# A decoder trunk step on one core: own buffers for one weight stream, a longer load lead, other spacing of side work

## The chip, the core and the metric

The kernel runs on one core of a Trainium2 chip. The core has five engines with queues of their own: TensorE (PE in the profile; its weight loads are listed as PEld), VectorE (DVE), ScalarE (ACT), GpSimd (POOL) and SyncE (SP). Each queue runs in order: an instruction that waits for a semaphore holds up everything behind it on that queue. SP and POOL only start transfers here, apart from a few memsets on POOL. The metric is device microseconds of one execution, from three runs; lower is better.

## The reference

One layer of a hybrid decoder trunk, for 256 prompt tokens and 8 single sample tokens at a model width of 2048, all in float32. What is computed, cut down:

```python
mod = silu(c) @ w_ada + b_ada                    # 2048 x 12288: six vectors of 2048 for each of 9 rows
sh1, sc1, gt1, sh2, sc2, gt2 = split(mod, 6)
h = rmsnorm(x, g_pre_mix) * (1 + sc1) + sh1
z = h @ w_in                                     # 2048 x 15376
y_a = u * (W_s v + b)                            # causal 128x128 mixing, 8 groups
y_b = head_rmsnorm(recurrence(q, k, v, log_f)) * silu(hg)    # HGRN2, 8 heads of 128x128 state
y_c = head_rmsnorm(recurrence(q, k, v, log_a)) * silu(gr)    # GLA, 4 heads of 128x256 state
merged = sum over n of sigmoid(z_gate[n]) * (y_n @ w_branch[n])
x = x + gt1 * rmsnorm(merged @ w_out, g_post_mix)
h2 = rmsnorm(x, g_pre_mlp) * (1 + sc2) + sh2
x = x + gt2 * rmsnorm(square(relu(h2 @ w_mlp_up)) @ w_mlp_down, g_post_mlp)   # 2048 -> 8192 -> 2048
```

The prompt starts from zero states; each sample has its own old states (`state_hgrn`, `state_gla`), which are loaded, decayed, added to and stored again. The outputs are the new rows, the final states of the prompt, the updated states of the samples and the normalised v rows of the samples.

## The kernel before, in words

**Products.** Activations lie transposed, 128 channels by 264 columns (256 prompt tokens and 8 samples). Every float32 weight tile is split into a high part (`whi`, a cast on ScalarE, line 108) and a rest (`wlo`, a subtraction on VectorE, line 105), and each product is made as three TensorE products: high by high, high by low, low by high (lines 534 to 536). The weights are walked in blocks of 512 KB. The work on one block is a *granule*: 24 products of 128x128 weights with 264 columns. `linear` runs four granules (two for `w_branch`) into one accumulator of two PSUM banks, of which there are two (`new_acc`), and calls `background()` after each.

**The stream of weights.** `plan()` lists all blocks in the order of use, and `Stream` loads and splits them ahead: on each call of `ahead()` (lines 507 to 516) blocks up to `at + SPLIT_AHEAD` (2) are split and blocks up to `at + LOAD_AHEAD` (3) are loaded by SP into tiles of the pool tag `raw`, which has `RAW_BUFS` (6) buffers of 512 KB. There are six pairs of `whi`/`wlo` halves, three blocks' worth. Blocks 20 to 71 are loaded in pairs with longer rows (lines 483 to 493).

**The first projection.** `CHUNKS = (2, 2, 4, 4, 4)` cuts the 16 tiles of the inner dimension into five chunks, and for each chunk all 20 column groups are run (lines 660 to 687). In the first two chunks a granule covers two inner tiles and 512 columns, so it needs both accumulators at once; its result is copied out (chunk 0, line 672, ScalarE) or added (later chunks, line 674, VectorE). For each next chunk `First.paced` loads the modulation's weights for that chunk into tiles of another pool (`blk`, line 380), runs its small TensorE products (line 257) between granules, and makes the modulated activations.

**The rest of the modulation.** `ada_round(r)` (lines 271 to 299) makes one of the vectors of `mod`: 16 steps, each of them four 512-column products (line 287, eight records in the trace) on two tiles of 512 KB. The next step's two tiles are requested right after a step (line 288); they come from the same tag `raw` as the stream's blocks (line 278). Rounds 2, 3 and 4 run during the mixers. Round 5 runs between the output projection and the MLP, with 12 of its 32 tiles loaded early into other buffers (lines 1311 to 1319).

**Side work.** The mixers' work is written as Python generators which are advanced after each granule: `bg` (the recurrences of the prompt, `mixer_r`), `bs` (the samples' states, `samples_r`) and `ba` (the modulation). A rate says how many units each may advance in a granule (`RATES`, in the order bg, bs, ba). Products of the side work that read results of other engines are held back and put between two granules by `slot()` (lines 541 to 570): it takes noted `levels` and `samples` that were noted in an earlier granule, and one step of `ba` if that has credit (`owed`). `background()` opens a slot when `ba.owed` has reached 0.9, or when something noted waits and `ba` has credit, or when it has waited three granules.

**The samples.** `samples_r` (lines 927 to 975) has 8 steps for each of two HGRN2 groups and 16 for the GLA group. A step loads a 256 KB tile of states (`st`, line 942, four buffers) and a 256 KB broadcast of values (`vbc`, line 944, two buffers) through POOL, scales on ScalarE (line 959), adds on VectorE (line 961), stores (line 962) and leaves the tile for TensorE (line 561).

**Who sets the order.** TensorE, SP and POOL are issued in the order of the program text up to line 688; after line 811 TensorE and POOL are, and SP is ordered by a planner that puts an instruction into its queue when its model says that inputs and buffers are there, earlier program text first. ScalarE and VectorE are always ordered by that planner, and after line 1256 all engines are. Once planned, each queue is fixed.

Of the kernel before, what the change touches and what calls it, by code (L numbers as in the profile page):

```python
# [7 lines left out]
F32 = mybir.dt.float32  # L8
# [7 lines left out]
P = 128  # L16
# [4 lines left out]
NT = NP + NS  # L21
# [7 lines left out]

KC = 4  # L30
CW = 256
RAW_BUFS = 6
SPLIT_BUFS = 6
NBLK = 28
CHUNKS = (2, 2, 4, 4, 4)
RATES = ((1.6, 0.4, 0.36), (1.42, 0.4, 0.36), (1.2, 0.4, 0.36), (1.0, 0.4, 0.36))
ST_BUFS = 4
VB_BUFS = 2
N_PRE = 12
PRE_AT = (2, 3, 4, 5)  # L40
R0 = 0.34
ADA_BATCH = 4
ADA_LEAD = 3
PAIRED = 72
LOAD_AHEAD = 3
SPLIT_AHEAD = 2
N_BRANCH = 3
FILL = (5.0, 9.0)
# [2 lines left out]
SLOT_WAIT = 3  # L51
HELD_OWED = 1.0
LEVELS_HELD = 3


@with_exitstack
def hybrid_step_kernel(
# [9 lines left out]
    V, S, T = nc.vector, nc.scalar, nc.tensor  # L67
# [3 lines left out]
    rawp = ctx.enter_context(tc.tile_pool(name="rawp", bufs=RAW_BUFS))  # L71
# [9 lines left out]
    def nm(s):  # L81
        uid[0] += 1
        return f"{s}_{uid[0]}"
# [8 lines left out]
    def tmp(shape, tag, bufs=2):  # L92
        return tp.tile(shape, F32, tag=tag, name=nm(tag), bufs=bufs)
# [177 lines left out]
    def ada_round(r, pre=()):  # L271

        acc = pada.tile([P, 512], F32, tag="ada", name=nm("ada"))

        def load(n):
            if n < len(pre):
                return pre[n]
            w = rawp.tile([P, 1024], F32, tag="raw", name=nm("raw"))
            c0 = r * D + n % 2 * 1024
            nc.sync.dma_start(w, w_ada[0, n // 2 * P:(n // 2 + 1) * P, c0:c0 + 1024])  # L280
            return w

        ws = [load(0), load(1)]
        yield
        for k in range(KT):
            for j in range(4):
                T.matmul(acc[32 * j:32 * j + 32, :], cT[:, k, :], ws[j // 2][:, j % 2 * 512:j % 2 * 512 + 512], start=k == 0, stop=k == KT - 1)  # L287
# [12 lines left out]

    now = [0]
# [173 lines left out]
    class Stream:  # L475
# [5 lines left out]
        def load(self, i):  # L481
            w, k, n, c0, width = self.items[i]
            if i < PAIRED and n == 4:

                assert self.items[i + 1][1:4] == (k, n, c0 + width)
                self.raw[i], self.raw[i + 1] = [], []
                for h in range(2):
                    t = rawp.tile([P, 2, 2 * width], F32, tag="raw", name=nm("raw"))
                    r0 = (k + 2 * h) * P
                    nc.sync.dma_start(t, w[r0:r0 + 2 * P, c0:c0 + 2 * width].rearrange("(k p) c -> p k c", p=P))  # L490
                    self.raw[i].append(t[:, :, 0:width])
                    self.raw[i + 1].append(t[:, :, width:2 * width])
                return
            t = rawp.tile([P, n, width], F32, tag="raw", name=nm("raw"))
            nc.sync.dma_start(t, w[k * P:(k + n) * P, c0:c0 + width].rearrange("(k p) c -> p k c", p=P))
            self.raw[i] = [t[:, 0:n // 2, :], t[:, n // 2:n, :]]
# [28 lines left out]
    def granule(w, k0, n, c0, width, accs, xh, xl, k, first, last):  # L525

        item, parts = stream[0].next()
        assert item[1:] == (k0 + k, n, c0, width)
        h = n // 2
        for j in range(n):  # L530
            for m in range(width // P):
                o = accs[m // 2][:, m % 2, 0:NT]
                a, b = (p[:, j % h, m * P:(m + 1) * P] for p in parts[j // h])
                T.matmul(o, a, xh(k + j), start=first and j == 0, stop=False)  # L534
                T.matmul(o, a, xl(k + j), start=False, stop=False)  # L535
                T.matmul(o, b, xh(k + j), start=False, stop=last and j == n - 1)  # L536
        stream[0].ahead()

    levels, samples = [], []

    def slot():

        lv = [x for x in levels if x[0] < now[0]][:2]
        sv = [x for x in samples if x[0] < now[0]]
        del levels[:len(lv)]
        del samples[:len(sv)]
        if lv:
            pl = sm([P, 2, 8, 32])
            for i, (_, lhs, rhs, _) in enumerate(lv):
                for h in range(4):  # L550
                    for hf in range(2):
                        for b in range(4):
                            t0 = hf * P + b * 32
                            T.matmul(pl[32 * b:32 * b + 32, i, 2 * h + hf, :], lhs[:, h, t0:t0 + 32], rhs[:, h, t0:t0 + 32], start=True, stop=True)  # L554
        if sv:
            G, qm, os_ = sv[0][1]
            nh = 512 // G.dv
            po = sm([P, G.dv])
            for h in range(4):
                for i, (_, _, b, sts) in enumerate(sv):  # L560
                    T.matmul(po[32 * h:32 * h + 32, :], qm[:, h, b, :], sts[h // nh][:, h % nh, :], start=i == 0, stop=i == len(sv) - 1)
        if ba.g and ba.owed >= 0.0:
            ba.step()
        for i, (_, _, _, put) in enumerate(lv):
            put(pl[:, i])
        if sv:
            if sv[0][2] == 0:
                V.tensor_copy(os_, po)
            else:
                add(os_, os_, po)  # L570

    def background():

        now[0] += 1
        bg.pump(rate[0])
        bs.pump(rate[1])
        ba.owed = min(ba.owed + rate[2], SLOT_LATE) if ba.g else 0.0
        wait = now[0] - min([x[0] for x in levels + samples] + [now[0]])
        if ba.owed >= SLOT_LATE or wait and (ba.g and ba.owed >= 0.0 or wait >= SLOT_WAIT):
            slot()  # L580

# [345 lines left out]
    def samples_r(G):  # L927
# [10 lines left out]
        ahead = []  # L938
# [12 lines left out]
        sts = []  # L951
        for n, (b, h0) in enumerate(steps):
            if n + 2 < len(steps):

                yield lambda: len(sts) + sum(len(x[3]) for x in samples) <= ST_BUFS - 3
                fetch(*steps[n + 2])
            st, v = ahead.pop(0)
            for i in range(nh):
                S.activation(st[:, i, :], st[:, i, :], AF.Copy, scale=fs[:, h0 + i, b:b + 1])  # L959
            for i in range(nh):  # L960
# [311 lines left out]
    parts = []  # L1272
# [179 lines left out]
```

## Time and profile before

| | us |
|---|---|
| three runs: lowest, median, highest | 2011.64, 2017.7, 2018.89 |
| the profiled execution, device time | 2011.83 |
| its span, first to last instruction | 2010.0 |
| TensorE busy | 1932.7 (96%) |
| VectorE busy | 1191.7 (59%) |
| ScalarE busy | 996.0 (50%) |
| GpSimd busy | 85.5 (4%) |

The mean granted TensorE clock was 0.985 and 442.05 MB were moved, 220 GB/s over the span. The profile's page gives busy times, the span in 40 slices, DMA queues, the chain that ended last, groups of instructions by line, and DMA issues. Other views of the same trace list who waited for whom, instructions in order of time, and sums over stretches. The end of a TensorE product is modelled, so a busy TensorE may still run at less than its best rate: the number of products in a stretch says more than its busy time.

By the trace, the first projection runs from about 31 us to 320 us, the three branches with their side work to about 1110 us, the output projection to about 1209 us, and the MLP from about 1241 us to the end.

### The profile page before, as it was taken

To read this page: it belongs to the slowest core of one execution; us is meant where nothing else is said; L and a number is where in the kernel's file an instruction comes from. 1 tells how busy PE (TensorE), PEld (TensorE's weight loads), DVE (VectorE), ACT (ScalarE), POOL (GpSimd) and SP (SyncE) were. 2 spreads that over 40 slices of the span, in tenths; PEclk is the share of its full clock that TensorE was granted. 3 is DMA by queue.
4 is the path that set the end of the run, shared out by engine and by line. 5 is a ranking of instruction groups with operands and counts; after the bars stand their busy time and mean duration, and the time that the engine had idled before them with its cause. 6 is when DMAs were issued, how large, how long until landed. Compare 5 with 4: busy or idle time off the path is not lost.

```text
span 2010.0 us, 42078 instructions
## 1 busy us (share of the span) xinstructions
PE 1932.7 (96%) x16972; PEld 1820.7 (91%) x16972; DVE 1191.7 (59%) x2095; ACT 996.0 (50%) x1773; POOL 85.5 (4%) x128
## 2 busy tenths in 40 slices
PE   6999999989998999989999999999999999999997
PEld 4889999879987988779999995999999999999996
DVE  3466667667566576445655556555555555555666
ACT  5444354546665664454544545555444444454543
POOL 1000000111011011220000000000000000000000
PEclk8999999999999999999999999999999999999998
DMA  9796787788799679886755766755555555555552
GB/s 343 253 333 238 254 286 235 219 249 250 234 288 257 202 229 287 258 263 192 223 184 180 268 204 219 231 180 179 180 183 182 180 179 182 181 183 179 179 178 75
DMA packets 341267, 442.05 MB, mean 220 GB/s; under 512 B 14930, under 2 KB 285008, under 8 KB 341072
## 3 DMA queue, kind: packets, MB, share of 16 engines
q1 hardware_dynamic: 330880, 409.19, 62.6%
q0 software_dynamic: 9120, 28.91, 6.1%
q8 instruction: 133, 2.18, 0.4%
q10 hardware_dynamic: 1072, 1.25, 0.2%
q14 instruction: 62, 0.51, 0.1%
HBM read 427.60 MB, written 11.70 MB: 219 GB/s over the span
## 4 chain that ended last, share of the span: by engine, by line
PE 82%; DMA 6%; issue 3%; DVE 2%; ACT 1%; POOL 0%; DVEq 0%; ACTq 0%; POOLq 0%; SPq 0%
PE mm L534 25%; PE mm L535 25%; PE mm L536 25%; PE ada L287 3%; DMA raw<-in_w_in_dram 2%; DMA vbc<-vs_d 1%; PE ada L257 1%; DVE wlo L105 1%; PE sm L695 1%; DMA raw<-in_w_ada_dram 1%; PE sm L1063 1%; DMA st<-in_state_hgrn_dram 0%; ACT whi L108 0%; PE sm L554 0%; DMA raw<-in_w_branch_dram 0%
## 5 line engine op out<-in xcount | busy, mean ns | idle before, releaser
L534 PE MATMUL mm<-b,whi 128*128 128x264 f32 x4624 | 1328.9, 287 | 15.9 <-ACT whi L108 6.5
L535 PE MATMUL mm<-b,whi 128*128 128x264 f32 x4624 | 1319.8, 285 | 0.2 <-DVE b L105 0.2
L536 PE MATMUL mm<-b,wlo 128*128 128x264 f32 x4624 | 1316.8, 285 | 3.0 <-DVE wlo L105 2.9
L105 DVE TENSOR_TENSOR wlo<-raw,whi 128x512 fp32r<-128x512 f32 x1156 | 792.8, 690 | 649.7 <-ACT whi L108 644.7
L108 ACT CAST whi<-raw 128x512 fp32r<-128x512 f32 x1156 | 708.8, 618 | 843.0 <-PE mm L535 699.6
L534 PEld LDWEIGHTS mm<-b,whi 128*128 128x128 f32 x4624 | 874.0, 189 | 71.5 <-issue 30.2
L536 PEld LDWEIGHTS mm<-b,wlo 128*128 128x128 f32 x4624 | 873.5, 189 | 4.8 <-DVE wlo L105 4.7
L535 PEld LDWEIGHTS mm<-b,whi 128*128 128x128 f32 x4624 | 873.4, 189 | 2.3 <-DVE b L105 1.4
L102 DVE TENSOR_TENSOR b<-b,mm 128x528 f32<-128x528 f32 x136 | 95.4, 704 | 39.3 <-PE mm L536 39.1
L287 PE MATMUL ada<-raw,cT 128*32 128x512 f32 x464 | 75.7, 640 | 3.7 <-DMA raw<-in_w_ada_dram 3.7
L961 DVE SCALAR_TENSOR_TENSOR st<-vbc,b,st 128x128 f32<-128x128 f32 (+1 forms) x96 | 33.9, 392 | 52.4 <-DMA vbc<-vs_d 39.3
L959 ACT ACTIVATE st<-st,fs 128x128 f32<-128x128 f32 (+1 forms) x96 | 36.4, 430 | 44.9 <-DMA st<-in_state_gla_dram 26.9
L257 PE MATMUL ada<-b,cT 128*32 128x256 f32 (+1 forms) x640 | 36.4, 364 | 9.9 <-DMA b<-in_w_ada_dram 9.2
L257 PEld LDWEIGHTS ada<-b,cT 128*32 128x32 f32 x640 | 18.3, 116 | 22.9 <-DMA b<-in_w_ada_dram 7.6
L99 DVE TENSOR_TENSOR b<-b,b 128x512 f32<-128x512 f32 (+1 forms) x47 | 33.7, 744 | 1.7 <-ACT b L1024 0.7
L287 PEld LDWEIGHTS ada<-raw,cT 128*32 128x32 f32 x464 | 13.2, 113 | 16.8 <-DMA raw<-in_w_ada_dram 8.6
L944 POOL DMA_DIRECT2D vbc<-vs_d x32 | 24.1, 754 | 77.7 <-DVE st L961 45.5
L105 DVE TENSOR_TENSOR b<-gt,b 128x528 fp32r<-128x528 f32 x32 | 22.7, 709 | 3.7 <-ACT whi L108 0.5
L962 POOL DMA_DIRECT2D out_dram<-st x32 | 23.5, 734 | 30.6 <-DVE st L961 15.9
L99 DVE TENSOR_TENSOR gt<-vt 128x528 f32<-128x528 f32 x32 | 22.5, 702 | 0.0
L105 DVE TENSOR_TENSOR b<-b 128x1024 f32<-128x1024 f32 (+1 forms) x21 | 22.3, 1067 | 0.1
L554 PE MATMUL sm<-b 128*32 128x32 f32 x960 | 11.9, 205 | 10.3 <-DVE b L99 10.3
(283 smaller groups left out, 783.0 us busy)
## 6 DMA issues: line engine op xcount, KB each, us to landing
raw<-in_w_in_dram SPq DMA_DIRECT2D x242, 512.0 KB, 5.6
raw<-in_w_mlp_up_dram SPq DMA_DIRECT2D x128, 512.0 KB, 3.9
raw<-in_w_mlp_down_dram SPq DMA_DIRECT2D x128, 512.0 KB, 3.6
raw<-in_w_ada_dram SPq DMA_DIRECT2D x116, 512.0 KB, 4.7
b<-in_w_ada_dram SPq DMA_DIRECT2D x60, 512.0 KB, 7.5
raw<-in_w_branch_dram SPq DMA_DIRECT2D x48, 512.0 KB, 5.2
raw<-in_w_out_dram SPq DMA_DIRECT2D x32, 512.0 KB, 3.7
b<-in_w_ada_dram SPq DMA_DIRECT2D x32, 256.0 KB, 6.6
```

Source lines behind the costliest of these rows:

```text
L99: V.tensor_tensor(o, a, b, op=ALU.mult)
L102: V.tensor_tensor(o, a, b, op=ALU.add)
L105: V.tensor_tensor(o, a, b, op=ALU.subtract)
L108: S.copy(hi, src)
L257: T.matmul(acc[32 * j:32 * j + 32, 0:n], cT[:, k, :], w[:, n * j:n * j + n], start=k == 0, stop=k == KT - 1)
L287: T.matmul(acc[32 * j:32 * j + 32, :], cT[:, k, :], ws[j // 2][:, j % 2 * 512:j % 2 * 512 + 512], start=k == 0, stop=k == KT - 1)
L534: T.matmul(o, a, xh(k + j), start=first and j == 0, stop=False)
L535: T.matmul(o, a, xl(k + j), start=False, stop=False)
L536: T.matmul(o, b, xh(k + j), start=False, stop=last and j == n - 1)
L944: nc.gpsimd.dma_start(v, vs_d[G.i, h * nj:h * nj + 4, b, :].partition_broadcast(P))
L959: S.activation(st[:, i, :], st[:, i, :], AF.Copy, scale=fs[:, h0 + i, b:b + 1])
L961: V.scalar_tensor_tensor(st[:, i, :], v[:, i, :], k[:, h0 + i, NP + b:NP + b + 1], st[:, i, :], ALU.mult, ALU.add)
```

## The change

- The modulation's steps and (with `spare`) some of the paired stream loads get a tag of their own, `araw`, with two buffers; the stream's tag `raw` goes from six buffers to four.
- Blocks are requested five ahead of the current one, not three. Splitting stays two ahead.
- The third rate goes from 0.36 to 0.27 (from 0.34 to 0.30 in the last chunk of the first projection); the first rates go from 1.6 and 1.42 to 1.7 and 1.5.
- `granule` runs all of its products for one accumulator, then those for the other. This differs from before only where there are two, in the first two chunks.
- `slot` takes only what was noted at least two granules ago, and what it counts as waiting is shifted by one granule with it.
- In `samples_r` the states are still requested two steps ahead, the values now one step ahead and by a function of their own, and a step's use comes at least three granules after the later of its two requests.

```diff
-RAW_BUFS = 6
+RAW_BUFS = 4
+ADA_RAW = 2
...
-RATES = ((1.6, 0.4, 0.36), (1.42, 0.4, 0.36), (1.2, 0.4, 0.36), (1.0, 0.4, 0.36))
+RATES = ((1.7, 0.4, 0.27), (1.5, 0.4, 0.27), (1.2, 0.4, 0.27), (1.0, 0.4, 0.27))
...
-R0 = 0.34
+R0 = 0.3
...
-LOAD_AHEAD = 3
+LOAD_AHEAD = 5
...
+FETCHED = 3
+AGE = 2
...
@@ ada_round, load(n)
-            w = rawp.tile([P, 1024], F32, tag="raw", name=nm("raw"))
+            w = rawp.tile([P, 1024], F32, tag="araw", name=nm("araw"), bufs=ADA_RAW)
...
@@ Stream.load, paired blocks
+                spare = i % 6 == 4 and i < PAIRED - 20
                 for h in range(2):
-                    t = rawp.tile([P, 2, 2 * width], F32, tag="raw", name=nm("raw"))
+                    if spare:
+                        t = rawp.tile([P, 2, 2 * width], F32, tag="araw", name=nm("araw"), bufs=ADA_RAW)
+                    else:
+                        t = rawp.tile([P, 2, 2 * width], F32, tag="raw", name=nm("raw"))
...
@@ granule
-        for j in range(n):
-            for m in range(width // P):
-                o = accs[m // 2][:, m % 2, 0:NT]
+        for acc0, m0 in [(acc, 2 * i) for i, acc in enumerate(accs)]:
+            for j in range(n):
+                for m in range(m0, min(m0 + 2, width // P)):
+                    o = acc0[:, m % 2, 0:NT]
...
@@ slot
-        lv = [x for x in levels if x[0] < now[0]][:2]
-        sv = [x for x in samples if x[0] < now[0]]
+        lv = [x for x in levels if x[0] + AGE <= now[0]][:2]
+        sv = [x for x in samples if x[0] + AGE <= now[0]]
...
@@ background
-        wait = now[0] - min([x[0] for x in levels + samples] + [now[0]])
+        wait = max(now[0] + 1 - AGE - min([x[0] for x in levels + samples] + [now[0]]), 0)
...
@@ samples_r
         def fetch(b, h):
             st = tmp([P, nh, dv], "st", ST_BUFS)
             nc.gpsimd.dma_start(st, G.s_in(b, h, nh))
+            ahead.append((st, now[0]))
+
+        def values(b, h):
             v = tmp([P, 4, P], "vbc", VB_BUFS)
             nc.gpsimd.dma_start(v, vs_d[G.i, h * nj:h * nj + 4, b, :].partition_broadcast(P))
-            ahead.append((st, v.rearrange("p (h j) v -> p h (j v)", h=nh)))
+            vals.append((v.rearrange("p (h j) v -> p h (j v)", h=nh), now[0]))
...
+        values(*steps[0])
+        yield
...
                 fetch(*steps[n + 2])
-            st, v = ahead.pop(0)
+            if n + 1 < len(steps):
+                values(*steps[n + 1])
+            yield lambda: now[0] >= max(ahead[0][1], vals[0][1]) + FETCHED
+            st, v = ahead.pop(0)[0], vals.pop(0)[0]
```

More of the change, by code (lines that the diff above doesn't have):

```diff
@@ L529, in granule @@
         h = n // 2
-        for j in range(n):
-            for m in range(width // P):
-                o = accs[m // 2][:, m % 2, 0:NT]
[L533 to L536, printed above, removed]
+        for acc0, m0 in [(acc, 2 * i) for i, acc in enumerate(accs)]:
+            for j in range(n):
+                for m in range(m0, min(m0 + 2, width // P)):
+                    o = acc0[:, m % 2, 0:NT]
+                    a, b = (p[:, j % h, m * P:(m + 1) * P] for p in parts[j // h])
+                    T.matmul(o, a, xh(k + j), start=first and j == 0, stop=False)
+                    T.matmul(o, a, xl(k + j), start=False, stop=False)
+                    T.matmul(o, b, xh(k + j), start=False, stop=last and j == n - 1)
         stream[0].ahead()
@@ L937, in samples_r @@
         steps = [(b, h) for b in range(NS) for h in range(0, 4, nh)]
-        ahead = []
+        ahead, vals = [], []
         def fetch(b, h):
```

## The prediction

> **What bounds the kernel now.** I read the page's busy times first, then busy time by stretch, to find where TensorE runs at its full pace and where not; then TensorE's waits, and for each large one what held up the engine it waited for.
>
> ```profile
> span 2010.0 us, 42078 instructions
> ...
> PE 1932.7 (96%) x16972; PEld 1820.7 (91%) x16972; DVE 1191.7 (59%) x2095; ACT 996.0 (50%) x1773; POOL 85.5 (4%) x128
> ```
> ```profile
> 0.00:50.00 50.00, 31.15 (x268) 23.11 (x272) 18.62 (x59) 25.64 (x45) 6.48 (x16) 0.90 1.02 342
> ...
> 118.00:123.00 5.00, 5.00 (x31) 5.00 (x30) 2.61 (x4) 1.31 (x3) 0.00 (x0) 0.66 0.97 329
> 1300.00:1900.00 600.00, 600.00 (x4940) 600.00 (x4940) 344.31 (x510) 288.96 (x477) 0.00 (x0) 1.00 0.57 181
> ```
>
> The second fence gives, for a stretch: its length, busy time and count of PE, PEld, DVE, ACT, POOL, the granted clock, the DMA share and GB/s. From 1300 to 1900 us TensorE has no gap: 600/4940 = 0.1215 us for a product, 24 x 0.1215 = 2.92 us for a granule. Nothing in the change makes a product cheaper, so gains lie only in TensorE's waits, most of which fall before 960 us:
>
> ```profile
> PE sm L554 <- DVE b L99: 10.3, 2, 6.1
> PE sm L1149 <- ACT b L1151: 6.9, 1, 6.9
> PE mm L534 <- ACT whi L108: 6.5, 3, 4.2
> PE sm L561 <- ACT b L1089: 4.3, 1, 4.3
> PE mm L536 <- DVE wlo L105: 2.9, 6, 1.4
> PE sm L784 <- DVE srow L780: 2.2, 1, 2.2
> PE ada L287 <- DMA raw<-in_w_ada_dram: 1.5, 3, 0.8
> ```
>
> These are the waits from 300 to 960 us (total, times, longest), 34.6 us together. ScalarE and VectorE are half idle over the span, so why are they late? Their queues stand still behind transfers, as ScalarE's waits and its order of time in the same stretch show:
>
> ```profile
> ACT whi L108 <- DMA raw<-in_w_in_dram: 62.0, 22, 8.7
> ACT st L959 <- DMA st<-in_state_gla_dram: 26.9, 9, 5.6
> ACT st L959 <- DMA st<-in_state_hgrn_dram: 18.0, 8, 8.1
> ```
> ```profile
> 420.61 0.40 ACT L959 ACTIVATE st<-st,fs 128x128 f32<-128x128 f32 x1 [8.08 <-DMA st<-in_state_hgrn_dram]
> ```
> ```profile
> 626.22 1.14 ACT L108 CAST whi<-raw 128x512 fp32r<-128x512 f32 x2 [3.62 <-DMA raw<-in_w_in_dram]
> ```
> ```profile
> 732.51 0.62 ACT L108 CAST whi<-raw 128x512 fp32r<-128x512 f32 x1 [6.27 <-DMA raw<-in_w_in_dram]
> ```
>
> The last two precede the two waits at line 554 (10.3 us); the first precedes the 4.2 us wait at line 534. Why the stream's block was late at 732 us stands in SP's queue:
>
> ```profile
> 711.31 0.46 SPq L495 DMA_DIRECT2D raw<-in_w_in_dram  x1
> 717.50 1.51 SPq L280 DMA_DIRECT2D raw<-in_w_ada_dram  x2
> 720.70 4.99 SPq L495 DMA_DIRECT2D raw<-in_w_in_dram  x3
> ```
>
> SP stood 6 us before two modulation loads which wanted a buffer of the shared tag, and the block behind them was requested only at 720.70 and reached ScalarE at 732.51, 11.8 us later. A modulation step and the next one's loads together can hold four of the six buffers, which leaves the stream two.
>
> **The change part by part.** *Accumulators in turn.* In the first two chunks a granule uses both accumulators, and both are finished only in its last quarter, so the next granule waits for their copies:
>
> ```profile
> 63.53 0.28 PE L536 MATMUL mm<-b,wlo 128*128 128x264 f32 x1
> 63.92 0.39 PE L534 MATMUL mm<-b,whi 128*128 128x264 f32 x1
> ...
> 65.48 0.39 PE L534 MATMUL mm<-b,whi 128*128 128x264 f32 x1 [0.57 <-ACT b L672]
> ```
> ```profile
> 61.00:75.00 14.00, 13.05 (x95) 11.68 (x93) 7.39 (x16) 9.40 (x18) 0.00 (x0) 1.00 0.88 316
> ```
>
> From 61 to 75 us no modulation step runs: 95 products at 0.1215 are 11.5 us, a few transposes about 0.55, so 14.0 - 11.5 - 0.55 = 1.9 us are lost in four granules, 0.48 each. With one accumulator done at half time, its copy has 1.46 us while the other half runs. Of 20 granules six are followed by modulation steps, which cover the copies already: 14 x 0.48 = 6.7 us gained. At the end of chunk 1 there is one long wait:
>
> ```profile
> 117.60 0.36 PE L534 MATMUL mm<-b,whi 128*128 128x264 f32 x1 [1.84 <-DVE b L102]
> ```
>
> It costs 1.84 us and then (31 products in the 5 us from 118, where 41 fit) 10 x 0.1215 = 1.2 us more, because the clock fell to 0.66. VectorE was late there with splits bunched behind late blocks; I count half of 3.0, 1.5 us. The opposite end: with four buffers and five blocks of lead, SP's fixed order puts loads that wait for a split ahead of chunk 2's modulation loads.
>
> ```profile
> 68.49 22.76 SPq L380 DMA_DIRECT2D b<-in_w_ada_dram  x8
> 91.34 2.44 SPq L495 DMA_DIRECT2D raw<-in_w_in_dram  x4
> ```
>
> Before, SP held the blocks back until 91.34 behind modulation loads that lacked a buffer; now modulation loads start later and blocks earlier. 512 KB at the 342 GB/s of the first stretch take 1.5 us; two transfers too late would cost 3 us. Ends: 14 x 0.48 and all of 3.0, or up to 20 x 0.48 + 3.0 = 12.6 gained; 3 lost. I take 8.2, since DMA runs at 0.88 of its time there, not at 1.
>
> *Own buffers and lead in the side-work stretch.* The stream always keeps four buffers, and a modulation load waits for its own two. The waits behind late blocks are L554 (10.3), L1149 (6.9), L561 (4.3) and the rest of L534 (6.5 - 4.2 = 2.3): 23.8 us. Each is followed by slower work, as a modulation step in a quiet place and one after a wait show:
>
> ```profile
> 264.01 1.06 PE L287 MATMUL ada<-raw,cT 128*32 128x512 f32 x8
> 265.00 0.39 PE L534 MATMUL mm<-b,whi 128*128 128x264 f32 x1
> ```
> ```profile
> 631.65 1.96 PE L287 MATMUL ada<-raw,cT 128*32 128x512 f32 x8
> ```
>
> 0.9 us more, say 1.0 for each of four: 27.8 us. Ends: all, or none if DMA traffic rather than the queue made the blocks late. I take 0.8 of it, 22.2: without the 6 us stop the 11.8 us of that load are about the 4 x 2.92 = 11.7 us in which four buffers come round, and three granules split ahead (8.8 us) cover what is left of most. The two-granule age of `slot` works at the same waits (2.92 us more time for VectorE) and is not counted again.
>
> *Samples spaced.* 4.2 us at line 534, 2.9 at line 536 and 1.0 after them, 8.1, stand behind sample loads. `FETCHED` moves the use in the text, but ScalarE and VectorE are ordered by a planner and may take it when the model says that data is there. Ends 0 and 8.1; I take half, 4.0.
>
> *The modulation's cost.* Its 48 steps in this stretch are the same 1.0 us each. What is new: with two buffers, a step's loads start only after the step before. Following the queues' rules granule by granule (0.27 credit each, a step costs 1, a slot opens at 0.9 or, at credit 0 and above, when something is two granules old), three steps come one granule after the last, four come two after, three come three after, the others four or more; for example credit reaches 0.9 at granule 28, the step leaves it at -0.1, and at 29 it is 0.17 while another level is old enough.
>
> ```profile
> raw<-in_w_mlp_up_dram SPq DMA_DIRECT2D x128, 512.0 KB, 3.9
> ...
> raw<-in_w_ada_dram SPq DMA_DIRECT2D x116, 512.0 KB, 4.7
> ```
>
> The second tile of a pair lands after about 4.7 + 1.5 = 6.2 us: 3 x (6.2 - 2.9) + 4 x (6.2 - 5.8) = 11.5 us of new waits, less the 1.5 of such waits now: +10.0. Ends: -1.5 if other products of the slots cover it; +58 if every pair takes the 11.8 us seen above (3 x 8.9 + 4 x 6.0 + 3 x 3.0 = 59.7, less 1.5). The median is the nearest row. No side queue ends late by the same count, from the first granule after the first projection: the first two groups finish at granule 96 (needed at 98) before and after, the GLA group at 157 (needed at 162), the rounds at 204 of 210. The lower rate moves steps to where the branches run without samples, at the same cost. Slots rise from 53 to 58: 5 x (0.39 - 0.12) = +1.4.
>
> *Between output projection and MLP.* Round 5 fills a chain of norms from 1209 to 1241 us. With six shared buffers seven steps on streamed tiles were hidden there; with two, one step per 6.2 us follows after the preloaded six (6.4 us): five fit. Two move into the MLP, 2.1 us, and a wait such as
>
> ```profile
> 1221.20 1.86 PE L287 MATMUL ada<-raw,cT 128*32 128x512 f32 x4 [2.24 <-DMA raw<-in_w_ada_dram]
> ```
>
> may double, 2: +4.1 (ends -2.2, that wait gone; +12, two steps at 6.2 in the chain).
>
> *Fewer buffers in the MLP.* A buffer returns every 4 x 2.92 = 11.7 us; split (two halves, 1.46 apart), and 3.9 to land are below 8. ScalarE's waits from 1300 to 1900 us show no transfer at all:
>
> ```profile
> ACT whi L108 <- PE mm L535: 284.9, 352, 1.3
> ACT whi L108 <- DVE wlo L105: 26.0, 31, 0.8
> ```
>
> So 0. [...]
>
> **Sum.** -8.2 - 22.2 - 4.0 + 10.0 + 1.4 + 4.1 = -18.9; 2011.8 - 18.9 = **1993 us**. The profiled execution is 5.9 us under the median of the runs (2017.7), so against that median the gain would look larger.
>
> [...]
>
> **Rivals.** (a) *All late transfers go*: the modulation's waits hide behind other products and samples are on time: -12.6 - 27.8 - 8.1 + 1.4 + 4.1 - 1.5 = -44.5, 1967 us. For it: three waits behind transfers explain most of the list; against it: 11.8 us for one block while samples load. (b) *Blocks stay late*, since DMA and not SP's queue sets them: no change from own buffers, 2011.8 - 8.2 + 10 + 1.4 + 4.1 - 4.0 = 2015; without new modulation waits 2005, so about 2010. (c) *The modulation waits for its own loads*, the other side: if a pair needs 10 us, 3 x 7.1 + 4 x 4.2 + 3 x 1.2 = 41.7, less 1.5, and 2011.8 - 34.4 + 40.2 + 5.5 = 2023 us. It decides from about 8.9 us a pair (7 x 8.9 - 31.9 = 30.4). (d) *A repeating gap in the MLP* for want of buffers: 256 blocks by 0.15 us for a gap of one product and more = 38 us, 2031 us; it needs a landing of over 7 us where 3.9 is the median. (e) *Spacing does nothing*, the planner undoes it: 4 us less gain, 1997 us.
>
> **How the numbers follow.** Chances: forecast 0.52, (a) 0.18, (b) 0.13, (c) 0.09, (d) 0.03, (e) 0.05. Half a per cent, 10 us, is about what a measurement here can tell from no change. Faster: 0.52 + 0.18 + 0.05 = 0.75, and 0.03 of (b), 0.78; same 0.10; slower (c) and (d), 0.12. The range goes from (a), 1967, to 2014, which takes in (b) and leaves out (c) and (d); the forecast's own is 1978 to 2004.
>
> **What would show it.** Right: no wait of TensorE at line 672's copies in the first two chunks; ScalarE's 62.0 us behind the stream cut to a third; waits at lines 554, 1149 and 561 under 1 us; waits of line 287 for its loads up, to about 11 us. Wrong: stream loads still late under a free buffer, modulation pairs landing after 9 us, or gaps in the MLP.

## The result: 0.8% slower, and the profile after

The changed kernel takes 2031.9 us (median; 2029.7 to 2032.9), the kernel before 2014.7 us measured beside it: a ratio of 1.0083, 95% interval 1.0057 to 1.011. The prediction was 1993 us, faster, with 1967 to 2014 as its range. Size and sign were wrong. The profiled execution takes 2031.4 us, 19.6 more than the one shown of before.

Lines have moved by 3 to 16 in the changed kernel: before's 287 is 290, 280 is 283, 534 to 536 are 542 to 544, 554 is 562, 1149 is 1165, 108 is 111, 495 is 502. In the kernels of the experiments they differ again by a few. The page first, with the group of the modulation's streamed products (instructions, then busy us and mean ns, then idle time before them):

```profile
span 2029.6 us, 42046 instructions
...
PE 1946.7 (96%) x16972; PEld 1823.7 (90%) x16972; DVE 1191.6 (59%) x2094; ACT 998.4 (49%) x1773; POOL 85.5 (4%) x128
...
L290 PE MATMUL ada<-araw,cT 128*32 128x512 f32 x464 | 89.3, 650 | 30.7 <-DMA araw<-in_w_ada_dram 30.6
```

The same row of the kernel before, and a step of it in the MLP, from its products in order of time:

```profile
L287 PE MATMUL ada<-raw,cT 128*32 128x512 f32 x464 | 75.7, 640 | 3.7 <-DMA raw<-in_w_ada_dram 3.7
```
```profile
1252.24 1.06 PE L287 MATMUL ada<-raw,cT 128*32 128x512 f32 x8
```

464 products in both, but the changed kernel waits 26.9 us more before them and is busy 13.6 us longer with them: 40.5 us on one line, twice the loss. All else together is some 21 us quicker. (A step of the modulation is eight of these records.) TensorE's waits from 300 to 960 us, after (total, times, longest):

```profile
PE ada L290 <- DMA araw<-in_w_ada_dram: 23.6, 10, 7.5
PE sm L1103 <- DVE b L102: 4.8, 1, 4.8
PE sm L562 <- DVE b L102: 3.8, 1, 3.8
PE sm L792 <- DVE srow L788: 1.8, 1, 1.8
PE sm L1165 <- ACT b L1167: 1.7, 1, 1.7
```

and ScalarE's in the same stretch:

```profile
ACT st L975 <- DMA st<-in_state_gla_dram: 28.4, 12, 5.6
ACT st L975 <- DMA st<-in_state_hgrn_dram: 27.1, 9, 5.3
...
ACT whi L111 <- DMA raw<-in_w_in_dram: 13.8, 6, 3.9
```

The waits on VectorE and ScalarE, which the prediction wanted to remove, fell from 33.1 us to 12.6 (two small rows are left out above); ScalarE's 62.0 behind the stream fell to 13.8. In their place stand 23.6 us in which TensorE waits for the modulation's own weights. The worst one, TensorE and SP's queue in order of time:

```profile
574.45 1.06 PE L290 MATMUL ada<-araw,cT 128*32 128x512 f32 x8
...
578.58 0.76 PE L562 MATMUL sm<-b,b 128*32 128x32 f32 x64
586.82 3.56 PE L290 MATMUL ada<-araw,cT 128*32 128x512 f32 x8 [7.48 <-DMA araw<-in_w_ada_dram]
```
```profile
577.09 3.58 SPq L502 DMA_DIRECT2D raw<-in_w_in_dram  x2
580.75 1.53 SPq L283 DMA_DIRECT2D araw<-in_w_ada_dram  x2
582.38 1.56 SPq L502 DMA_DIRECT2D raw<-in_w_in_dram  x2
588.78 1.98 SPq L283 DMA_DIRECT2D araw<-in_w_ada_dram  x2
```

One step ends at 575.5; the next one stands one granule behind it. Its two buffers are free from 575.5 on, but SP is at two stream loads (577.09 and, at the end of that row, about 580.3) and requests the pair only at 580.75, 5.2 us late. The first tile lands 6 us later, at 586.8, 11.3 us after the step before. Then the step itself is slow, by the stretch's row (length, busy time and count of PE, PEld, DVE, ACT, POOL, granted clock, DMA share, GB/s; the second row is the MLP's):

```profile
586.00:592.00 6.00, 5.18 (x19) 2.06 (x20) 0.00 (x0) 0.00 (x0) 0.00 (x0) 0.59 0.91 292
1300.00:1900.00 600.00, 600.00 (x4940) 599.02 (x4939) 342.44 (x507) 287.76 (x474) 0.00 (x0) 1.00 0.59 181
```

The granted clock is 0.59, and the eight products take 3.56 us where 1.06 did at 574.45. So a wait of 7.48 us cost about 10.

The second loss is in the fill between output projection and MLP and just behind it:

```profile
1228.94 1.67 PE L290 MATMUL ada<-araw,cT 128*32 128x512 f32 x2 [4.03 <-DMA araw<-in_w_ada_dram]
...
1236.79 1.92 PE L290 MATMUL ada<-araw,cT 128*32 128x512 f32 x4 [1.62 <-DMA araw<-in_w_ada_dram]
...
1245.04 1.05 PE L290 MATMUL ada<-araw,cT 128*32 128x512 f32 x4
1246.84 1.05 PE L290 MATMUL ada<-araw,cT 128*32 128x512 f32 x4
```

Counted from the trace, 9 steps of round 5 run in the fill and 7 in the MLP (11 and 5 before). Five of those seven, and two of the five before, run as two halves at different times, as the two tiles of a pair land apart (1.3 us for the pair of the halves at 1264.30 and 1266.22, 4.5 us for that of 1270.44 and 1273.82): a half of four takes 1.05 us, as long as a whole step of eight does at 1252.24 in the kernel before. The output projection with its fill takes 4.2 us more and the MLP 7.1.

### The profile page after: what moved, and what is told of

It is laid out like the page before. It is cut to its first block, busy times and chain, and to the rows that moved or that the text cites. A ratio compares the mean times of both kernels' runs of the same rounds, so it can differ in the third digit from the quotient of the medians.

```text
span 2029.6 us, 42046 instructions
## 1 busy us (share of the span) xinstructions
PE 1946.7 (96%) x16972; PEld 1823.7 (90%) x16972; DVE 1191.6 (59%) x2094; ACT 998.4 (49%) x1773; POOL 85.5 (4%) x128
## 4 chain that ended last, share of the span: by engine, by line
PE 85%; DMA 9%; DVE 2%; issue 1%; ACT 1%; SPq 0%; POOL 0%; DVEq 0%; ACTq 0%; POOLq 0%
PE mm L542 26%; PE mm L543 25%; PE mm L544 25%; DMA araw<-in_w_ada_dram 4%; PE ada L290 4%; DMA vbc<-vs_d 2%; PE ada L260 1%; DMA b<-in_w_ada_dram 1%; DVE wlo L108 1%; PE sm L703 1%; ACT whi L111 1%; DMA raw<-in_w_in_dram 1%; DMA st<-in_state_gla_dram 0%; DMA b<-in_x_prompt_dram 0%; PE sm L562 0%
## 5 line engine op out<-in xcount | busy, mean ns | idle before, releaser
L108 DVE TENSOR_TENSOR wlo<-raw,whi 128x512 fp32r<-128x512 f32 x1136 | 778.0, 690 | 628.1 <-ACT whi L111 625.7
L111 ACT CAST whi<-raw 128x512 fp32r<-128x512 f32 x1136 | 696.8, 618 | 811.3 <-PE mm L543 719.9
L290 PE MATMUL ada<-araw,cT 128*32 128x512 f32 x464 | 89.3, 650 | 30.7 <-DMA araw<-in_w_ada_dram 30.6
L290 PEld LDWEIGHTS ada<-araw,cT 128*32 128x32 f32 x464 | 13.3, 111 | 51.3 <-DMA araw<-in_w_ada_dram 44.0
L111 ACT CAST whi<-araw 128x512 fp32r<-128x512 f32 x20 | 12.4, 621 | 21.6 <-PE mm L543 19.8
L108 DVE TENSOR_TENSOR b<-b 128x1024 f32<-128x1024 f32 (+1 forms) x21 | 22.4, 1069 | 1.0 <-PE sm L562 1.0
L102 DVE TENSOR_TENSOR gt<-vt 128x528 f32<-128x528 f32 x32 | 22.4, 700 | 0.0
```

The lines of the kernel that those rows point to most:

```text
L102: V.tensor_tensor(o, a, b, op=ALU.mult)
L108: V.tensor_tensor(o, a, b, op=ALU.subtract)
L111: S.copy(hi, src)
```

## Experiments

Two theories stood at the start. Theory 1: the modulation's ring of two makes each step wait for loads that begin only after the step before. Theory 2: the rate, age and lead move side work to dearer places, and the buffers are innocent. The stage times, taken from the first product of each stage in each kernel's profiled execution, are in the table after the runs.

**One ring again.** After the change, with shared buffers:

```diff
-RAW_BUFS = 4
+RAW_BUFS = 6
...
-            w = rawp.tile([P, 1024], F32, tag="araw", name=nm("araw"), bufs=ADA_RAW)
+            w = rawp.tile([P, 1024], F32, tag="raw", name=nm("raw"))
```
(and the same for the stream's blocks that borrowed `araw`)

> All of the change stays but the own buffers: the modulation's loads and the stream's take turns in one shared ring of six again. Theory 1 (the ring of two makes each modulation step wait for loads that start only after the step before): the waits of TensorE at line 290 on the modulation's loads, 30.6 us in the profile of the changed kernel, fall under 5 us, and about 25 to 35 us of the time go, less what comes back of the waits behind late stream blocks (up to 20): 2000 to 2020 us. Theory 2 (the lower rate, the two-granule age and the longer lead move side work to dearer places, and the buffers are not the cause): the time stays at 2025 to 2035 us and the waits only change their line.

Measured: 2015.4 us, 1.0008 of before [0.9994, 1.0022]. Its waits from 300 to 960 us:

```profile
PE ada L290 <- DMA raw<-in_w_ada_dram: 22.0, 7, 7.5
PE sm L1103 <- DVE b L102: 5.3, 1, 5.3
```

The loss in the fill went for the most part (output projection and MLP 120.7 and 763.2 us; before 121.8 and 761.1), but the mixers' waits stayed. So theory 1 holds for the fill, where steps follow at once, and misses for the mixers; that the time lies in its range is luck, since the gain came from other stages. Six buffers did not help the mixers beside a lead of five blocks; whether the lead is why, the fifth run asks.

**Own buffers alone**, on the kernel before: `RAW_BUFS = 4`, `ADA_RAW = 2` and the tag `araw` for the modulation's tiles and the `spare` blocks, nothing else.

> The kernel before with one edit: four buffers for the stream and two of its own for the modulation. Rate, lead, age, order of the products as before. Theory 1: the rate of 0.36 spaces the modulation's steps closer than 0.27 did, so the waits of TensorE on modulation loads come to 30 us or more, and the time is 15 to 40 us above the kernel before, though the waits behind late stream blocks (23.8 us before) get shorter. Theory 2: no slower than the kernel before, since the parts that cost are left out.

Measured: 2045.7 us, 1.0151 [1.0119, 1.0183]. Waits from 300 to 960 us:

```profile
PE ada L288 <- DMA araw<-in_w_ada_dram: 31.6, 14, 6.0
PE sm L1154 <- ACT b L1156: 5.9, 1, 5.9
PE sm L559 <- DVE b L100: 3.3, 1, 3.3
PE sm L789 <- DVE srow L785: 1.8, 1, 1.8
```

As theory 1 said. The own buffers alone are the dearest part of the change, and theory 2 falls. They did cut the other waits to 11 us; whether by the buffers or because TensorE, standing 31.6 us elsewhere, gave VectorE that time, this run can't tell.

**Accumulators in turn alone**, on the kernel before:

```diff
-        for j in range(n):
-            for m in range(width // P):
-                o = accs[m // 2][:, m % 2, 0:NT]
+        for acc0, m0 in [(acc, 2 * i) for i, acc in enumerate(accs)]:
+            for j in range(n):
+                for m in range(m0, min(m0 + 2, width // P)):
+                    o = acc0[:, m % 2, 0:NT]
...
```

> The kernel before with one edit: the products of a granule go accumulator by accumulator. Both theories: 4 us faster (what the first projection took less in the changed kernel: 1.9 + 1.2 + 0.7 + 0.6), where the prediction had 8.2; after the first five chunks nothing changes, as one accumulator is used there. 2009 to 2012 us beside 2014.7.

Measured: 2004.1 us, 0.9949 [0.9933, 0.9964]; the first projection is 10.1 us shorter. More than expected, and what the prediction's own terms give if all of the long wait goes: 6.7 + 3.0 = 9.7. In the first two chunks this kernel is 9.5 us quicker than before, the changed one 3.1: the rest of the change takes 6 us of it back there.

**Steps further apart.** After the change, with one rule in `slot()`:

```diff
+ADA_GAP = 3
...
-    levels, samples = [], []
+    levels, samples, ada_at = [], [], [-9]
...
-        if ba.g and ba.owed >= 0.0:
+        if ba.g and ba.owed >= 0.0 and now[0] - ada_at[0] >= ADA_GAP:
+            ada_at[0] = now[0]
```

> The changed kernel with one rule more: a slot takes a modulation step only if three granules (8.8 us) or more have passed since the last one. Buffers, rate, lead and age as in the changed kernel. Theory 1 in its narrow form (a pair of loads lands some 6 to 10 us after the step before, and only the steps that follow within two granules wait): the waits at line 290 within the mixers, some 23 us of the 30.6, fall under 8 us, and the time falls by 15 to 25 us, to 2007 to 2017; the waits in the fill ahead of the MLP, 7.4 us, stay. Theory 2: no change beyond 3 us, as the number of steps and slots stays. A third reading (SP's queue holds the pair back behind stream loads, so that it lands late however far apart the steps are): the waits stay above 15 us.

Measured: 1990.3 us, 0.9881 [0.9857, 0.9906], 41.6 us below the changed kernel. Waits from 300 to 960 us:

```profile
PE ada L291 <- DMA araw<-in_w_ada_dram: 3.5, 3, 2.7
PE sm L563 <- DVE b L103: 2.5, 1, 2.5
PE sm L1167 <- ACT b L1169: 1.8, 1, 1.8
PE sm L794 <- DVE srow L790: 1.8, 1, 1.8
```

This settles the mixers: same buffers, lead, rate and number of steps, only the distance between steps differs, and 20 of the 23.6 us of waits are gone with it. More went than expected (15 to 25). In the mixers it is 37.3 us: 29.0 around the steps, more than the waits, since a wait had also slowed the step behind it, and 8.3 elsewhere, where the waits for VectorE and ScalarE got shorter too. In the changed kernel seven steps follow the last one within two granules (three at one, four at two); here none does.

**One ring, lead of three.** The first experiment with `LOAD_AHEAD = 3`:

> As the first experiment (one shared ring of six), and the stream's lead back from five blocks to three; rates, age, spacing of samples and order of products as in the changed kernel. The first experiment kept 22 us of waits on modulation loads in the mixers with a shared ring. Reading A (the distance between two steps is the cause, whatever the ring): with a lead of three the steps stand at the same granules, so the waits stay near 22 us and the time at 2010 to 2018 us. Reading B (the lead is part of it: with a lead of five the shared ring is full of the stream's blocks, so a pair is requested only when a split has freed a buffer; with three SP can request it before the step ahead of it has run): the waits fall under 8 us and the time to 1990 to 2000 us, unless waits behind late stream blocks come back.

Measured: 2002.3 us, 0.9946 [0.9927, 0.9965]; waits on modulation loads from 300 to 960 us:

```profile
PE ada L290 <- DMA raw<-in_w_ada_dram: 8.0, 4, 3.9
```

This is reading B, though a little outside its numbers (8.0 us of waits, and 2002 rather than 2000): with the steps at the same granules, a shared ring that the stream doesn't fill lets SP request a pair earlier. So the lead was why the first experiment kept its waits. That fits the kernel before, whose steps also come close together (one at one granule, ten at two) and which hardly waits.

**The fourth kernel again** (the lead in it is five):

> The fourth experiment's kernel once more, for its spread: 1988 to 1993 us.

Measured: 1988.2 us in a single run, as expected.

**The fill, first try.** The fourth kernel, with round 5's tiles taken from the stream's four buffers.

> The fourth experiment (steps three granules apart) and one edit: round 5, which fills the chain of norms ahead of the MLP, loads its tiles into the stream's ring of four instead of the two own buffers. Theory 1: two own buffers let one step follow per round trip of a load; with four a second pair is under way, the waits of 3.8 and 1.6 us in the fill go, and 3 to 7 us of the 1990 us go with them. Rival: the MLP's first blocks then wait for those buffers, and the same time is lost at the MLP's first products: 1988 to 1993 us.

Measured: 1990.5 us, 0.9876 [0.9839, 0.9913]: no gain clear of the spread (one of the four runs took 1980.5), the rival. A new row of ScalarE's waits shows the price:

```profile
ACT whi L112 <- DMA raw<-in_w_mlp_up_dram: 24.2, 11, 8.8
```

The MLP's first blocks now stand behind round 5, the MLP takes 771.3 us instead of 767.6, and 8 instead of 7 steps fall into it.

**The fill, second try.** The fourth kernel with more of round 5 loaded early:

```diff
-N_PRE = 12
+N_PRE = 20
```

> The fourth experiment and one edit: 20 instead of 12 of round 5's tiles are loaded far ahead, into buffers of their own. Theory 1: four steps more of the fill need no load in time, so the waits of 3.8 and 1.6 us there go: 3 to 7 us less than 1990. Rival: the added 4 MB of early loads delay the first projection, where DMA is busy for 0.88 of the time (eight tiles of 512 KB at 342 GB/s are 12 us of DMA time): no gain or up to 8 us slower.

Measured: 1975.8 us, 0.9816 [0.9797, 0.9835], 14.5 below the fourth, twice the upper end of what was expected. Twelve steps now run in the fill and four in the MLP: output projection and fill 120.6 us, MLP 761.1, together 10.1 us less than in the fourth. The expectation had counted the waits and forgotten the halves in the MLP. The mixers' 4.2 us less are about what two executions of the fourth kernel differ by (763.1 and, in its second run, 759.1).

**The lead alone.** After the change, `LOAD_AHEAD = 3`:

> The changed kernel with one edit: the stream's lead is three blocks again instead of five; own buffers, rates, age and order as in the changed kernel, so the steps stand at the same granules. In the changed kernel the step at 586.82 us waited 7.5 us: its pair's buffers were free when the step before ended, at 575.5, but SP, which takes its loads in order, stood at stream loads that wanted a buffer (issued at 577.09 and 580.29) and requested the pair only at 580.75; it landed 6.0 and 6.5 us later. Theory 1a (the long lead keeps SP standing ahead of the pair, and that is about half of the wait): with a lead of three SP requests the pair as soon as the step before ends, the mixers' waits at line 290 fall from 23 us to about 12, and the time to 2012 to 2022 us. Theory 1b (the round trip of the ring of two is all of it, and the lead does not matter): waits of 20 us or more and 2025 to 2035 us.

Measured: 2030.7 us, 1.0091 [1.0066, 1.0116]. Theory 1a fell and the numbers of 1b came: the waits at line 290 from 300 to 960 us are 24.8. SP's queue shows why, at the place of the 7.48 us wait:

```profile
572.82 3.57 SPq L502 DMA_DIRECT2D raw<-in_w_in_dram  x2
576.49 1.43 SPq L283 DMA_DIRECT2D araw<-in_w_ada_dram  x2
```

The step before ends at 571.3 there, and SP, still at stream loads, requests the pair 5.2 us later, as with the lead of five. That fits a stream ring of four in which a load waits for a split whatever the lead says; a kernel with more buffers for the stream beside the two own ones wasn't tried.

**Lead of three with spaced steps and early tiles.** The eighth kernel with `LOAD_AHEAD = 3`:

> The eighth experiment (own buffers, steps three granules apart, 20 tiles of round 5 loaded ahead) and a lead of three instead of five. In the fifth experiment, with the lead of three, the first two chunks took 9.1 us less than before; with the lead of five they took 5 us less. If that difference is the lead's, 4 us go: 1970 to 1973 beside 1975.8. Against it, waits behind late stream blocks can come back, up to 20 us: up to 1995.

Measured: 1971.7 us, 0.981 [0.9788, 0.9833]. The intervals of the eighth and this one overlap; the first projection is 3.2 us shorter.

**The same with one shared ring** (the two edits of the first experiment):

> The tenth kernel with one edit: one shared ring of six for the stream and the modulation instead of four and two of its own. If own buffers are worth something once the steps stand three granules apart (stream blocks no longer late behind modulation loads), this is 8 us or more slower than the tenth, with more of ScalarE's waits for stream blocks. If the distance of the steps was all that mattered, it is within 4 us of the tenth.

Measured: 1971.0 us, 0.9796 [0.978, 0.9811]. ScalarE's waits from 300 to 960 us, first here, then in the tenth kernel:

```profile
ACT whi L112 <- DMA raw<-in_w_in_dram: 55.9, 24, 5.6
```
```profile
ACT whi L112 <- DMA raw<-in_w_in_dram: 16.3, 10, 3.1
```

ScalarE waits 40 us more for blocks, and the median is the same. TensorE's waits from 300 to 960 us on everything but the modulation's loads sum to 15 us here and to 8 in the tenth, where the kernel before, under the same kind of ring, had 33. In the profiled executions the mixers are 9.7 us longer here and the other stages 4.9 shorter. So own buffers may be worth up to some 10 us in the mixers, which they lose elsewhere; TensorE's waits fell to less than half of before's without them and without the longer lead. What else had removed the waits?

**Samples not spaced**, on the tenth kernel (`FETCHED = 0`):

> The tenth kernel with one edit: FETCHED is 0, so a sample's state is used as soon as the work's order comes to it and not three granules after its load. The prediction gave the spacing 4.0 us (half of 8.1). If it is right: ScalarE's waits for sample loads grow by several us and the time by 3 to 5, to 1975 to 1977. Rival (the spacing does nothing, since ScalarE waits for about as long either way and TensorE does not wait for it): within 2 us of the tenth, 1970 to 1974.

Measured: 1977.1 us, 0.9836 [0.9814, 0.9858], 5.4 us above the tenth; the two intervals overlap, so a loss is likely and its size open. ScalarE's waits for the GLA states rise from 29.2 to 40.9, those for the HGRN2 states fall from 28.9 to 25.9. The prediction's 4.0 is in reach, but TensorE loses the time at other places than thought:

```profile
PE ada L291 <- DMA araw<-in_w_ada_dram: 9.2, 7, 3.6
```

from 0.7 in the tenth, while the waits at lines 563 and 1167 are no longer than there. The steps are no closer than there, so pairs land later. SP's queue is part of it: the pair of the step at 749.61 was requested at 739.31, 8.3 us after the step before had ended. What held the loads up stays open.

**Age of one granule**, on the tenth kernel (`AGE = 1`):

> The tenth kernel with one edit: AGE is 1, so a slot takes up a level or a sample one granule after it was put down, as in the kernel before, and not two. The prediction counted nothing for the age beside the own buffers. If that is right: within 3 us of the tenth (1969 to 1975), and TensorE's waits at lines 563, 1167 and 545 stay near 6 us in sum. Rival (the age is what keeps VectorE and ScalarE in time): those waits come back to 15 us and more, and 8 to 20 us are lost, 1980 to 1992.

Measured: 1996.1 us, 0.9928 [0.99, 0.9955], 24.3 us above the tenth. From 300 to 960 us:

```profile
PE sm L563 <- DVE b L103: 13.1, 3, 8.1
PE sm L1167 <- ACT b L1169: 6.1, 1, 6.1
```
```profile
710.00:722.00 12.00, 4.37 (x79) 4.34 (x80) 11.62 (x17) 4.58 (x9) 0.00 (x0) 0.57 0.80 256
```

The second fence is the stretch around the 8 us wait: VectorE is busy for 11.62 of 12 us, TensorE for 4.37, at a clock of 0.57. Own buffers and both kinds of spacing are there, and the waits at before's lines 554 and 1149 are back.

**The same under the shared ring** (the eleventh with `AGE = 1`):

> The eleventh kernel (one shared ring of six) with the same edit, AGE 1. In the eleventh ScalarE waits 78 us for stream blocks and TensorE hardly for ScalarE. If the age of two granules is what covers late blocks there, it is lost now: 10 to 25 us slower than the eleventh, 1981 to 1996, with waits of TensorE for VectorE's and ScalarE's results of 15 us and more. If the distance of the modulation's steps alone was enough: within 4 us of the eleventh.

Measured: 1992.7 us, 0.9914 [0.9891, 0.9936], 21.7 above the eleventh. With the steps spaced, the age of two granules is worth 22 to 24 us under either ring. It isn't enough by itself: the fifth kernel has it, with one ring, a lead of three and steps not spaced, and TensorE's waits there on everything but the modulation's loads still sum to 23 us.

| kernel | us (median) | first projection | mixers | output projection and fill | MLP |
|---|---|---|---|---|---|
| before | 2014.7 | 289.5 | 788.7 | 121.8 | 761.1 |
| changed | 2031.9 | 285.1 | 800.4 | 126.0 | 768.3 |
| 1, one ring | 2015.4 | 282.5 | 798.7 | 120.7 | 763.2 |
| 2, own buffers alone | 2045.7 | 289.9 | 815.5 | 124.0 | 768.4 |
| 3, in turn alone | 2004.1 | 279.4 | 792.4 | 121.1 | 761.1 |
| 4, steps apart | 1990.3 | 283.4 | 763.1 | 124.2 | 767.6 |
| 5, one ring, lead 3 | 2002.3 | 278.8 | 791.4 | 121.6 | 760.8 |
| 7, as 4, fill from the stream's buffers | 1990.5 | 282.9 | 764.2 | 122.5 | 771.3 |
| 8, apart, 20 early tiles | 1975.8 | 284.7 | 758.9 | 120.6 | 761.1 |
| 9, changed, lead 3 | 2030.7 | 283.5 | 803.9 | 127.7 | 768.3 |
| 10, as 8, lead 3 | 1971.7 | 281.5 | 754.8 | 120.8 | 761.1 |
| 11, as 10, one ring | 1971.0 | 279.3 | 764.5 | 120.4 | 758.8 |
| 12, as 10, samples not spaced | 1977.1 | 281.4 | 765.4 | 120.4 | 761.1 |
| 13, as 10, age 1 | 1996.1 | 281.9 | 783.4 | 122.2 | 761.6 |
| 14, as 11, age 1 | 1992.7 | 279.7 | 781.5 | 120.5 | 759.5 |

Beside the groups of runs the kernel before was measured at 2011.5 to 2014.7 us. The tenth and eleventh are about 2% faster than the kernel before and, through it, 3% faster than the changed one.

## Why the prediction was wrong

*Modulation's cost, +10.0: the step that failed.* The count was exact: three steps come one granule after the last, four come two after, three come three after. The price was wrong. The prediction let the pair land 4.7 + 1.5 = 6.2 us after the step before, which takes for granted that SP is free to request it at once. SP was at stream loads, and the first tile of the pair landed 11.3 us after it at the worst place and 9.2 us after it at the step of 428.19 us:

```profile
410.70 12.52 SPq L502 DMA_DIRECT2D raw<-in_w_in_dram  x5
423.32 0.93 SPq L283 DMA_DIRECT2D araw<-in_w_ada_dram  x2
```
```profile
740.32 1.03 SPq L283 DMA_DIRECT2D araw<-in_w_ada_dram  x2
```

The step before that one ended at 418.9, 4.4 us ahead of the request. Only at the third such place was SP free (second fence): it requested the pair as the step before ended, at 741.0, and the first tile reached TensorE at 747.04, 6.0 us later, about as forecast. The prediction had seen such a queue in the trace of before (SP six us at a place, and 11.8 us from a block's request to ScalarE) and used it only as the far end of its range and in rival (c), which decides from 8.9 us a pair. And a wait was counted as idle time only: the step behind it also ran at a lower clock, or in two halves. From the last product before a step to the first one after it, start to start and summed over the mixers, the kernel before takes 57.6 us and the changed one 90.0: 32.4 more, not 10. The fourth run shows the cause, by removing it without touching the buffers.

Rival (c) named the mechanism and forecast 2023 us at a chance of 0.09. Its price for the modulation, 40.2 us, was above the 32.4 measured; it fell 8 us short because the fill lost more and the other parts gained less than forecast.

*Clock.* The granted clock was 0.59 in the stretch with the step behind the wait of 7.48 us. In the kernel before it fell as well (0.66 from 118 to 123 us), behind a wait of only 1.84 us. The forecast's +10.0 has no term for what a wait does to the step behind it. That step took 2.5 us more than a quiet one (3.56 for 1.06); at this price, an estimate from this one step, the three waits of 3.3 us would have added 7.5: nearer to the 32.4, though not near.

*Fill, +4.1, in truth +11.3.* Two steps moved into the MLP, just as forecast (by its first product the MLP of the kernel before begins at 1231 us and not at 1241, so five steps on streamed tiles ran ahead of it, not seven; now it is three). But the waits were 4.0 and 1.6 us where 2.2 stood before, and five of the seven steps in the MLP came in halves, where two of five did. Two steps, three more halved and a wait of 1.4 us at the step of 1270.44 are 6.6 of the MLP's 7.1 us. The upper end, +12, held.

*Own buffers and lead, -22.2, and samples, -4.0.* The waits went about as forecast: from 33.1 us to 12.6, and everything in the mixers but the modulation got 20.7 us quicker. Of the marks given, ScalarE's 62.0 fell to 13.8 (right), and before's waits at line 561 went, but 3.8 and 1.7 us stayed at lines 562 and 1165, before's 554 and 1149 (wrong: under 1 was forecast). That the sum came out near is in part luck, since the cause given was in the main another one. The last runs give it by parts, for the mixers without the time around the modulation's steps: 729.0 us with one ring and an age of one granule (the fourteenth), 722.0 with own buffers (the thirteenth), 712.8 with one ring and an age of two (the eleventh), 702.2 with both (the tenth). So with spaced steps own buffers are worth 7 to 11 us in the mixers, which the whole time doesn't show, and the age 16 to 20; each figure is from one execution, and two executions of one kernel differ by some 4. The prediction mentioned the age and counted nothing for it, as the buffers were to have done the same work. In the changed kernel itself, where TensorE stands 23.6 us at the modulation's loads and so gives the other engines time, the shares were not taken apart. The spacing of samples, 5.4 us with overlapping intervals, is not far from the 4.0, by another way than the one named.

*Accumulators in turn, -8.2, in truth -4.4.* Alone it is worth 10: the mechanism was right. From 61 to 75 us the changed kernel runs 112 products where the one before ran 95. The mark given, no wait at line 672's copies, did not quite come true: three such waits, 1.6 us, are left in the first two chunks, one of them (0.31 us at 65.97) in this stretch. And there is one long wait behind VectorE at 113.65 us:

```profile
61.00:75.00 14.00, 13.69 (x112) 13.48 (x111) 8.57 (x18) 10.83 (x20) 0.00 (x0) 1.00 0.52 151
```
```profile
113.65 0.56 PE L542 MATMUL mm<-b,whi 128*128 128x264 f32 x1 [2.74 <-DVE b L105]
```

The lead of five and the ring of four took back what it gained: 282.5 us with one ring and lead five, 281.5 with own buffers and lead three (in the tenth), 278.8 with one ring and lead three. The prediction's bad end had named a way, SP's order of loads, and SP's queue shows it, in the changed kernel and then in the third:

```profile
47.38 27.86 SPq L502 DMA_DIRECT2D raw<-in_w_in_dram  x9
75.29 4.82 SPq L383 DMA_DIRECT2D b<-in_w_ada_dram  x8
```
```profile
40.93 20.13 SPq L495 DMA_DIRECT2D raw<-in_w_in_dram  x9
61.11 5.54 SPq L380 DMA_DIRECT2D b<-in_w_ada_dram  x8
```

The changed kernel's SP is at stream loads until 75.2 us and requests the next modulation tiles 14 us later than the third's; from 61 to 75 us 151 GB/s move. That this order is what costs the 6 us, no run shows by itself.

*MLP with four buffers, 0*: right. 4940 products from 1300 to 1900 us, as before, with TensorE busy for all of the 600 us: no gap repeats, and rival (d) is out.

Summed up in the profiled executions: -4.4 + 11.7 + 4.2 + 7.1 = +18.6, of the 19.6 measured. From the forecast of -18.9 to the measured +19.6 it is 38.5 us: 22.4 for the modulation in the mixers, 7.2 for the fill, 3.8 for the accumulators, 4.1 for own buffers, samples and slots together, and 1.0 outside these stages.

## What to carry to other kernels

Here a private ring as deep as one step's loads hid no more than the distance to the step before, which is little if steps come in bunches: from the end of the step before to the landing it took 6.0 us where SP was free, and 9.2 and 11.3 us where it stood at other loads for 4.4 and 5.2 us of that. So read the issuing queue before giving a landing time. Spacing the steps by three granules took more of the waits (to 3.5 us, with the same two buffers) than the shared ring of six did (22.0 us with a lead of five, 8.0 with three), and no stage of that kernel was longer than in the changed one. When two parts of a change work on the same wait, undo each by itself before crediting one.

## What was unexpected of the hardware

Four of a step's eight modulation products take 1.05 us (1246.84) and all eight together take 1.06 (1252.24 before). So a step whose two tiles were used as they landed took 2.10 us of TensorE time, twice as much as one that had both; idle time that the halves may save is not in this. And the longest wait cost more than its length: 7.48 us idle, then 3.56 us for a step of 1.06, part of it a clock of 0.59 (586 to 592 us) and part the second tile, which landed 1.6 us after the first.
